# Layer-norm statistics behind a mixture in three parts, and POOL's share of the last norm in pieces of 256 columns

## The chip, the cores and the metric

The kernel runs on one core of a Trainium2 chip. The metric is the device time of one execution in microseconds (us). The engines are TensorE (PE, its weight loads are PEld), VectorE (DVE), ScalarE (ACT), GpSimd (POOL) and SyncE (SP), which here only issues DMA transfers.

## What is computed

Two decoder layers over 256 tokens of width 1024, batch 1, in float32. Layer 0 mixes the tokens with a sparse attention, layer 1 with a latent attention; both add a cross-attention into 256 memory tokens. Each half layer ends in a post-norm with residual, and each layer has a mixture of 16 experts. In short:

```python
DEEPNORM_ALPHA = (2.0 * DEPTH) ** 0.25
def layer_norm(x, g, b):
    mu = jnp.mean(xf, -1, keepdims=True)
    var = jnp.mean(jnp.square(xf - mu), -1, keepdims=True)
    y = (xf - mu) * lax.rsqrt(var + LN_EPS) * g + b
for i in range(DEPTH):
    ...
    x = layer_norm(DEEPNORM_ALPHA * x + y, ln_g[i, 0], ln_b[i, 0])
    f = hier_moe(x, moe_w_grp[i], moe_b_grp[i], moe_w_exp[i], moe_b_exp[i], moe_w_gate[i], moe_w_up[i], moe_w_down[i])
    x = layer_norm(DEEPNORM_ALPHA * x + f, ln_g[i, 1], ln_b[i, 1])
```

The change concerns the last line: the norm behind a mixture, once between the layers and once at the end of the kernel.

## The kernel before

**Tiles.** The 256 tokens are two tiles (t = 0, 1) of 128 partitions; the 1024 columns are two halves (h = 0, 1) of 512. `x_tm[:, t, h*512:...]` in SBUF holds the residual stream. The order of the instructions on each engine is the order in which the program writes them.

**The mixture** (`moe`) goes over eight pairs of experts (k = 0 to 7). For each pair PE multiplies by the gate and up matrices (`up`, L1606), then by the down matrix (L1780, for the last pair L1801). The outcome `yb` is split into a rounded part (ACT, L1807) and the rest (DVE, L1810), and `combine` (L1612, matmuls at L1615) adds both parts into `acc[t][hf]`, one PSUM bank of 512 columns for each tile and half. `acc[t][1]` already holds the residual of half 1, put in by PE (`add_x`), so half 1 is finished by matmuls alone; half 0 is added to `x_tm` by DVE (`resid`, L868), which also takes its statistics (`half_stats`, L875).

**The end of a mixture.** For the last pair, half 1 of the down product is done in two column blocks of 256, each with a PSUM bank of its own. Then DVE takes the statistics of half 0 of tile 1 (L1811), and PE issues `combine(7, 1, ...)` for columns 0 to 255 and 256 to 511: eight matmuls of 256 columns, in each block the rounded part for tiles 0 and 1, then the rest for tiles 0 and 1. `overflow` (L1625) follows: it loads a flag, and a block of code (L1637) runs only when an expert has too many tokens; every engine that has work in it passes the branch. From then on `z_(t, 1)` reads half 1 from `acc[t][1]`.

**The norm behind it.** `half_stats` writes six numbers per half into `lnst[t]`; `ln_stats` combines them (DVE, L908), adds epsilon (DVE, L909), and POOL raises the variance to the power -1/2 (L910) and makes the bias (L911). `norm` is two DVE instructions per half tile (L916, which needs the mean, and L917, which needs POOL's power). `norm_slow` does one half tile with ACT (L931) and two POOL instructions (L932 multiplies by the gain, L934 adds the bias).

**Between the layers** (`mla`, L1893 on): statistics of half 1 of tile 0, its norm, twelve warming matmuls on PE (`warm(12)`, L487), PE's transposes of that half tile (`xT`, L942), four more warming matmuls, then the same for tile 1, with the projection of layer 1 (L1888) behind the transposes.

**At the end** (`finish`, L2055): statistics of both tiles, `norm` of half 0 of tile 0, `norm_slow` of half 1 of tile 0, `norm` of half 0 and half 1 of tile 1. Each quarter of the output goes out by one DMA on SP's queue, in the order (0,0), (1,0), (0,1), (1,1), written as (tile, half); (0,1) is POOL's quarter.

Of the kernel before, what the change touches and what calls it, by code (L numbers as in the profile page):

```python
# [10 lines left out]
F32 = mybir.dt.float32  # L11
# [4 lines left out]
OP = mybir.AluOpType  # L16
# [3 lines left out]
P = 128  # L20
S = 256
D = 1024
NT = S // P
# [9 lines left out]
ALPHA = 4.0 ** 0.25  # L33
LN_EPS = 1e-5
# [74 lines left out]
def trunk(ctx: ExitStack, tc: tile.TileContext, A, out, dbg=None, layers=2, kb=ARENA_KB):  # L109
    nc = tc.nc  # L110
    PE, V, SC, G = nc.tensor, nc.vector, nc.scalar, nc.gpsimd
# [5 lines left out]
    work = ctx.enter_context(tc.tile_pool(name="work", bufs=2))  # L117
# [98 lines left out]
    def bank(name="pt"):  # L216
        return ps.tile([P, 512], F32, tag="ps", name=name)
# [420 lines left out]
    class Step:  # L638
# [46 lines left out]
        def norm(self, i):  # L685
            n0, sm = self.n0, self.sm[i]
            for t in range(NT):
                a, n = (0, n0) if t == 0 else (n0, S)
                v = self.p[i][:, a:a + n]
                if self.act:  # L690
                    SC.activation(v, v, AF.Copy, scale=sm[:, t:t + 1])
                else:
                    V.tensor_scalar(v, v, sm[:, t:t + 1], None, op0=OP.mult)
# [169 lines left out]
    lnst = {}  # L863

    def resid(t, h, yb, stats=True, f=ALPHA):

        z = x_tm[:, t, h * 512:(h + 1) * 512]
        V.scalar_tensor_tensor(z, z, f, yb, op0=OP.mult, op1=OP.add)  # L868
        if h == 0:
            lnst[t] = work.tile([P, 2, 6], F32, tag="lnst", name="lnst")  # L870
        if stats:
            half_stats(t, h)

    def half_stats(t, h):
        V.bn_stats(lnst[t][:, h, :], z_(t, h))  # L875

    def router_prep(l):

# [23 lines left out]
    def z_(t, h):  # L902
        return zps[t] if h and t in zps else x_tm[:, t, h * 512:(h + 1) * 512]

    def ln_stats(t, eps=LN_EPS):

        mv = lnmv[t] = work.tile([P, 5], F32, tag="lnmv", name="lnmv")
        V.bn_aggr(mv[:, 0:2], lnst[t])  # L908
        V.tensor_scalar(mv[:, 2:3], mv[:, 1:2], eps, None, op0=OP.add)  # L909
        G.tensor_tensor(mv[:, 3:4], mv[:, 2:3], mhalf, op=OP.pow)  # L910
        G.tensor_scalar(mv[:, 4:5], mv[:, 0:1], mv[:, 3:4], -1.0, op0=OP.mult, op1=OP.mult)  # L911
# [16 lines left out]
    def norm_slow(t, h, gb):  # L928

        z, mv = x_tm[:, t, h * 512:(h + 1) * 512], lnmv[t]  # L930
        SC.activation(z, z_(t, h), AF.Identity, bias=mv[:, 4:5], scale=mv[:, 3:4])  # L931
        G.tensor_tensor(z, z, gb[h][:, 0, :], op=OP.mult)  # L932
        yield
        G.tensor_tensor(z, z, gb[h][:, 1, :], op=OP.add)  # L934
        yield

    def xT(t, put, halves=(0, 1)):

# [420 lines left out]
    def out_tail(l):  # L1359
# [32 lines left out]
        for t in range(NT):  # L1392
            g_piece(l, 1, "b", 0, t)
            resid(t, 0, y[t, 0])
        for t in range(NT):
            xT(t, put, (0,))
            g_piece(l, 1, "b", 1, t)
        open_spare()
        resid(0, 1, y[0, 1])
        router(0, 0)  # L1400
        xT(0, put, (1,))
        resid(1, 1, y[1, 1], False)
        ln_stats(0)
        half_stats(1, 1)
        ln_stats(1)
        router(1, 0)
        xT(1, put, (1,))
# [99 lines left out]
    def moe(l, lg, lb, nxt):  # L1507
# [30 lines left out]
        def by4(v):  # L1538
            return v.rearrange("p (q c) -> p c q", c=4)
# [72 lines left out]
        def combine(k, hf, a=0, b=512):  # L1612
            for n in range(2):
                for t in range(NT):
                    PE.matmul(acc[t][hf][:, a:b], SkT[k % 2][:, t * P:(t + 1) * P], yhl[hf][n][:, a:b],  # L1615
                              start=(k == 0 and n == 0), stop=(k == 7 and n == 1 and b == 512), skip_group_check=True)
# [8 lines left out]
        def overflow():  # L1625


            go, gn = tmp("go", [P, NT, NE]), tmp("gn", [P, NT, NE - 1])
            xT = [tmp("oxT%d" % t, [P, KC, P]) for t in range(NT)]
            wt = [tmp("owt%d" % i, [P, 4, P]) for i in range(2)]  # L1630
            ho = tmp("ho", [P, S])
            wd = tmp("owd", [P, D])
            xs = tmp("oxs", [P, 512])
            zs = [tmp("ozs%d" % t, [P, 512]) for t in range(NT)]
            pg, yo = bank("pg"), bank("yo")
            flag = nc.values_load(over[0:1, 0:1], min_val=0, max_val=1)
            with tc.If(flag > 0):  # L1637
                V.scalar_tensor_tensor(go, rank, float(CAP), g16, op0=OP.is_gt, op1=OP.mult)
                for t in range(NT):
                    for c0 in range(0, KC, 4):  # L1640
                        xh, xl = [v[:, t, c0 * P:(c0 + 4) * P].bitcast(F32) for v in two[0]]
                        V.tensor_tensor(by4(xs), *[v.rearrange("p (c q) -> p c q", c=4) for v in (xh, xl)], op=OP.add)
                        for c in range(4):
                            PE.transpose(yo[:, c * P:(c + 1) * P], xs[:, c * P:(c + 1) * P], ident)
                        V.tensor_copy(xT[t][:, c0:c0 + 4, :], yo.rearrange("p (c t) -> p c t", c=4))
                    V.tensor_copy(zs[t], acc[t][1])
                with tc.For_i(0, NE, 1) as e:
                    with tc.For_i(0, FF // P, 1) as f:
                        for n, w in enumerate((A["moe_w_gate"], A["moe_w_up"])):
                            for hf in range(2):  # L1650
                                nc.sync.dma_start(wt[hf], w[l, bass.ds(e, 1), hf * 512:(hf + 1) * 512, bass.ds(f * P, P)]
                                                  .rearrange("o (c p) f -> p (o c) f", p=P))
                                for t in range(NT):
                                    for c in range(4):
                                        PE.matmul(pg[:, n * S + t * P:n * S + (t + 1) * P], wt[hf][:, c, :],
                                                  xT[t][:, 4 * hf + c, :], start=(n + hf + t + c == 0),
                                                  stop=(hf + c == 4), skip_group_check=True)
                        SC.activation(ho, pg[:, 0:S], AF.Silu)
                        V.tensor_tensor(ho, ho, pg[:, S:], op=OP.mult)
                        nc.sync.dma_start(wd, A["moe_w_down"][l, bass.ds(e, 1), bass.ds(f * P, P), :]  # L1660
                                          .rearrange("o p f -> p (o f)"))
                        for t in range(NT):
                            for hf in range(2):
                                z = zs[t] if hf else x_tm[:, t, 0:512]
                                PE.matmul(yo, ho[:, t * P:(t + 1) * P], wd[:, hf * 512:(hf + 1) * 512], start=True, stop=True)
                                V.scalar_tensor_tensor(z, yo, go[:, t, 0:1], z, op0=OP.mult, op1=OP.add)

                    V.tensor_copy(gn, go[:, :, 1:NE])
                    V.tensor_copy(go[:, :, 0:NE - 1], gn)
                for t in range(NT):  # L1670
                    V.tensor_copy(acc[t][1], zs[t])
                    half_stats(t, 0)
            ar.drop("go", "gn", "oxT0", "oxT1", "owt0", "owt1", "ho", "owd", "oxs", "ozs0", "ozs1")

        places(0)
# [17 lines left out]
        for k in range(8):  # L1693
# [52 lines left out]
            if k == first - 1:  # L1746
# [4 lines left out]
                for j in range(first, 8):  # L1751
                    i = j % 2
                    at[j] = (two[1][:, :, 2 * i:2 * i + 2, :],
                             lambda c, i=i: x2[c // 4][:, c % 4, i * P:(i + 1) * P])
# [55 lines left out]
                        V.tensor_tensor(yhl[hf][1][:, cs], yb[:, cs], yhl[hf][0][:, cs].bitcast(F32), op=OP.subtract)  # L1810
        half_stats(1, 0)  # L1811
        ar.drop("Sk", "Skg", "xg0", "h_sb")
        for a in (0, 256):
            combine(7, 1, a, a + 256)
        for t in range(NT):
            zps[t] = acc[t][1]

        overflow()
        ar.drop("rank", "g16")
# [34 lines left out]
    def mla(res):  # L1854
# [13 lines left out]
        gb = res["gb"]  # L1868
# [21 lines left out]


        SC.activation(kTb[0][:, 0, 0:1], mhalf, AF.Exp)
        half_stats(0, 1)  # L1893
        ln_stats(0, LN_EPS / ALPHA ** 2)
        norm(0, 0, gb)
        warm(12)
        xT(0, put, (0,))
        warm(4)
        split("mi1", hi=(SC, SC), lo=(None, None))
        half_stats(1, 1)  # L1900
        ln_stats(1, LN_EPS / ALPHA ** 2)
        split("mi1", hi=(None, None), lo=(G, G))
        norm(1, 0, gb)
        norm(0, 1, gb)
# [150 lines left out]
    def finish(res):  # L2055

        ov = out[0].rearrange("(t p) d -> p t d", p=P)
        gb = res["gb"]

        def put(t, h, z):  # L2060
            nc.sync.dma_start(ov[:, t, h * 512:(h + 1) * 512], z)

        for t in range(NT):
            half_stats(t, 1)
            ln_stats(t, LN_EPS / ALPHA ** 2)
        put(0, 0, norm(0, 0, gb))
        slow = norm_slow(0, 1, gb)
        next(slow)
        put(1, 0, norm(1, 0, gb))
        next(slow)  # L2070
        put(0, 1, x_tm[:, 0, 512:])
        put(1, 1, norm(1, 1, gb))
# [37 lines left out]
```

## Time and profile before

| | us |
|---|---|
| runs | 723.64, 723.23, 722.20 (median 723.23) |
| the profiled execution's own time | 723.13 |
| its span | 721.3 |
| PE busy | 695.8 (96%) |
| DVE, ACT, POOL busy | 278.8, 218.1, 157.7 |
| bytes moved by DMA | 235.58 MB, mean 327 GB/s |

The span runs from the first to the last record of the profile; the execution's own time lies 1.8 us above it. Busy time is the sum of an engine's instructions. Matmuls are pipelined, so a busy PE is not PE at its peak.

### The profile page before, as it was taken

To read this page: it belongs to the slowest core of one execution; us is meant where nothing else is said; L and a number is where in the kernel's file an instruction comes from. 1 tells how busy PE (TensorE), PEld (TensorE's weight loads), DVE (VectorE), ACT (ScalarE), POOL (GpSimd) and SP (SyncE) were. 2 spreads that over 40 slices of the span, in tenths; PEclk is the share of its full clock that TensorE was granted. 3 is DMA by queue.
4 is the path that set the end of the run, shared out by engine and by line. 5 is a ranking of instruction groups with operands and counts; after the bars stand their busy time and mean duration, and the time that the engine had idled before them with its cause. 6 is when DMAs were issued, how large, how long until landed. Compare 5 with 4: busy or idle time off the path is not lost. (4 is left out here: it accounts for less than half of the span.)

```text
span 721.3 us, 10956 instructions
## 1 busy us (share of the span) xinstructions
PE 695.8 (96%) x4122; PEld 414.5 (57%) x4122; DVE 278.8 (39%) x730; ACT 218.1 (30%) x528; POOL 157.7 (22%) x249
## 2 busy tenths in 40 slices
PE   7999999899999999999999999999999999999993
PEld 7999998777543435335344677776435334353342
DVE  4255587857621221021112776646403111211206
ACT  3365457673412101010121754443203011111011
POOL 5998645031301300000000640032103000000003
PEclk9999999999999999999999999999999999999997
DMA  9895875537879999999999994567899999999971
GB/s 298 255 277 167 277 296 165 216 146 276 310 274 420 387 383 417 419 421 420 419 419 369 389 408 164 205 237 266 342 364 420 418 419 420 422 418 418 420 245 60
DMA packets 66728, 235.58 MB, mean 327 GB/s; under 512 B 10923, under 2 KB 30446, under 8 KB 47214
## 3 DMA queue, kind: packets, MB, share of 16 engines
q1 hardware_dynamic: 66670, 234.82, 84.4%
q8 instruction: 34, 0.56, 0.3%
q14 instruction: 24, 0.20, 0.1%
HBM read 233.76 MB, written 1.05 MB: 326 GB/s over the span
## 5 line engine op out<-in xcount | busy, mean ns | idle before, releaser
L384 POOL TENSOR_TENSOR wl<-arena,wh 128x256 fp32r<-128x256 f32 (+4 forms) x108 | 91.2, 882 | 23.7 <-ACT wh L374 6.7
L1780 PE MATMUL yb<-arena 128*64 128x512 f32 x328 | 88.7, 595 | 0.0
L910 POOL TENSOR_TENSOR lnmv<-lnmv,mhalf 128x1 f32<-128x1 f32 x8 | 6.4, 805 | 359.6 <-DVE lnmv L909 359.3
L1730 DVE SCALAR_TENSOR_TENSOR arena<-arena,csb,u 128x512 f32<-128x512 f32 x16 | 12.0, 748 | 187.8 <-PE u L1606 106.7
L1606 PE MATMUL g<-arena 128*64 128x512 f32 x196 | 53.8, 593 | 0.0
L1785 DVE TENSOR_TENSOR y<-yb,y 128x512 fp32r<-128x512 f32 x28 | 19.4, 692 | 85.4 <-ACT y L1784 85.4
L1780 PEld LDWEIGHTS yb<-arena 128*64 128x64 f32 x328 | 27.3, 137 | 42.1 <-issue 40.9
L1606 PE MATMUL u<-arena 128*64 128x512 f32 x180 | 48.8, 593 | 0.0
L675 ACT ACTIVATE arena<-s,mx 128x128 f32<-128x128 f32 (+1 forms) x88 | 36.9, 430 | 35.2 <-DVE mx L669 35.2
L1784 ACT CAST y<-yb 128x512 fp32r<-128x512 f32 x28 | 16.4, 585 | 89.7 <-PE yb L1780 89.7
L1742 ACT COPY arena<-hT 128x256 f32<-128x256 f32 x16 | 6.0, 372 | 117.2 <-DVE arena L1742 117.2
L1606 PE MATMUL g<-arena,xg 128*64 128x512 f32 x144 | 39.7, 592 | 0.0
L1606 PE MATMUL u<-arena,xg 128*64 128x512 f32 x168 | 39.6, 592 | 0.0
L1780 PE MATMUL yb<-split,arena 128*64 128x512 f32 x112 | 39.4, 596 | 0.0
L1615 PE MATMUL acc<-y,SkT 128*128 128x512 f32 (+1 forms) x136 | 38.6, 406 | 0.0
L1720 ACT ACTIVATE arena<-g 128x512 f32<-128x512 f32 x16 | 9.6, 597 | 92.1 <-PE g L1606 92.0
L1615 PEld LDWEIGHTS acc<-y,SkT 128*128 128x128 f32 x136 | 22.6, 189 | 15.9 <-issue 12.9
L669 DVE TENSOR_REDUCE mx<-s 128x1 f32<-128x128 f32 (+1 forms) x88 | 27.2, 363 | 9.8 <-PE s L653 4.9
L1606 PEld LDWEIGHTS g<-arena 128*64 128x64 f32 x196 | 16.8, 137 | 23.3 <-issue 22.4
L1606 PEld LDWEIGHTS u<-arena 128*64 128x64 f32 x180 | 15.1, 137 | 23.6 <-issue 23.6
L1551 POOL TENSOR_TENSOR xl<-x_tm,xh 128x512 fp32r<-128x512 f32 x8 | 12.0, 1549 | 68.9 <-ACT xh L1550 68.9
L374 ACT CAST wh<-arena 128x1024 fp32r<-128x1024 f32 (+3 forms) x26 | 25.1, 999 | 3.8 <-DMA arena<-in_mem_w_kv_dram 2.8
(417 smaller groups left out, 1367.9 us busy)
## 6 DMA issues: line engine op xcount, KB each, us to landing
arena<-in_moe_w_down_dram SPq DMA_DIRECT2D x41, 1024.0 KB, 11.5
arena<-in_moe_w_up_dram SPq DMA_DIRECT2D x41, 1024.0 KB, 15.7
arena<-in_moe_w_gate_dram SPq DMA_DIRECT2D x35, 1024.0 KB, 15.6
arena<-in_moe_w_gate_dram SPq DMA_DIRECT2D x31, 512.0 KB, 7.8
split<-in_moe_w_down_dram SPq DMA_DIRECT2D x14, 1024.0 KB, 17.3
split<-in_moe_w_gate_dram SPq DMA_DIRECT2D x13, 1024.0 KB, 14.6
arena<-in_nsa_w_in_dram SPq DMA_DIRECT2D x7, 1024.0 KB, 8.0
arena<-in_moe_w_up_dram SPq DMA_DIRECT2D x14, 512.0 KB, 5.3
```

The costliest lines, as they stand in the source:

```text
L374: SC.copy(wh[:, c, :], t[:, c, :])
L384: lo[j].tensor_tensor(wl[:, d, :], t[:, d, :], wh[:, d, :].bitcast(F32), op=OP.subtract)
L669: V.tensor_reduce(self.mx[i][:, t:t + 1], v, axis=AX.X, op=OP.max, negate=True)
L675: SC.activation(self.p[i][:, a:a + n], self.sb[i][:, a:a + n], AF.Exp, bias=self.mx[i][:, t:t + 1], scale=1.0, accum_out=self.sm[i][:, t:t ...
L1551: G.tensor_tensor(zl, z, zh.bitcast(F32), op=OP.subtract)
L1606: PE.matmul(b_[e * 64:(e + 1) * 64, :], at[k][1](i * n + c)[:, e * 64:(e + 1) * 64], w_[e][:, c, :], start=(i + c == 0), stop=(i * n + c = ...
L1615: PE.matmul(acc[t][hf][:, a:b], SkT[k % 2][:, t * P:(t + 1) * P], yhl[hf][n][:, a:b], start=(k == 0 and n == 0), stop=(k == 7 and n == 1 a ...
L1720: SC.activation(h_sb, gp, AF.Silu)
L1730: V.scalar_tensor_tensor(h_sb, h_sb, gs[:, k % 2:k % 2 + 1], up_, op0=OP.mult, op1=OP.mult)
L1780: PE.matmul(yb[hf][e * 64:(e + 1) * 64, :], hT[:, 2 * q + c, e * 64:(e + 1) * 64], w_[e][:, c, hf * 512:(hf + 1) * 512], start=(q + c == 0 ...
L1784: SC.copy(yhl[hf][0], yb[hf])
L1785: V.tensor_tensor(yhl[hf][1], yb[hf], yhl[hf][0].bitcast(F32), op=OP.subtract)
```

## The change

Statistics of half 1 behind a mixture are taken in two instructions of 256 columns instead of one of 512, so `lnst[t]` has three groups of six numbers. Those of columns 0 to 255 stand directly behind the closing matmuls of these columns, in front of the matmuls of columns 256 to 511 and in front of the branch; those of columns 256 to 511 stay where the statistics of 512 were. In `norm_slow` POOL's multiplication and addition are each written as two instructions of 256 columns. Both layers have the first edit, the last norm alone the second.

```diff
-            lnst[t] = work.tile([P, 2, 6], F32, tag="lnst", name="lnst")
+            lnst[t] = work.tile([P, 3, 6], F32, tag="lnst", name="lnst")
...
-    def half_stats(t, h):
-        V.bn_stats(lnst[t][:, h, :], z_(t, h))
+    def half_stats(t, h, part=None):
+
+        i, z = (h, z_(t, h)) if part is None else (1 + part, z_(t, h)[:, part * 256:part * 256 + 256])
+        V.bn_stats(lnst[t][:, i, :], z)
...
-    def ln_stats(t, eps=LN_EPS):
+    def ln_stats(t, eps=LN_EPS, n=2):
...
-        V.bn_aggr(mv[:, 0:2], lnst[t])
+        V.bn_aggr(mv[:, 0:2], lnst[t][:, 0:n])
...
         SC.activation(z, z_(t, h), AF.Identity, bias=mv[:, 4:5], scale=mv[:, 3:4])
-        G.tensor_tensor(z, z, gb[h][:, 0, :], op=OP.mult)
-        yield
-        G.tensor_tensor(z, z, gb[h][:, 1, :], op=OP.add)
-        yield
+        for k, op in enumerate((OP.mult, OP.add)):
+            for c in (slice(0, 256), slice(256, 512)):
+                G.tensor_tensor(z[:, c], z[:, c], gb[h][:, k, c], op=op)
+            yield
...
                     V.tensor_copy(acc[t][1], zs[t])
                     half_stats(t, 0)
+                    half_stats(t, 1, 0)
...
         half_stats(1, 0)
         ar.drop("Sk", "Skg", "xg0", "h_sb")
-        for a in (0, 256):
-            combine(7, 1, a, a + 256)
         for t in range(NT):
             zps[t] = acc[t][1]
+        combine(7, 1, 0, 256)
+        for t in range(NT):
+            half_stats(t, 1, 0)
+        combine(7, 1, 256, 512)
...
-        half_stats(0, 1)
-        ln_stats(0, LN_EPS / ALPHA ** 2)
+        half_stats(0, 1, 1)
+        ln_stats(0, LN_EPS / ALPHA ** 2, 3)
         norm(0, 0, gb)
         warm(12)
...
-        half_stats(1, 1)
-        ln_stats(1, LN_EPS / ALPHA ** 2)
+        half_stats(1, 1, 1)
+        ln_stats(1, LN_EPS / ALPHA ** 2, 3)
...
         for t in range(NT):
-            half_stats(t, 1)
-            ln_stats(t, LN_EPS / ALPHA ** 2)
+            half_stats(t, 1, 1)
+            ln_stats(t, LN_EPS / ALPHA ** 2, 3)
```

## Rows read from the trace of the kernel before

**Rows 1.** Busy time by stretch: PE, PEld, DVE, ACT, POOL, PE clock, DMA share, GB/s.

```profile
610.00:630.00 20.00, 20.00 (x96) 7.77 (x94) 2.87 (x6) 1.92 (x4) 0.00 (x0) 1.00 1.01 421
```

**Rows 2.** Waits of PEld, 404 to 710 us: total us, times, longest.

```profile
PEld yb L1780 <- DMA arena<-in_moe_w_up_dram: 0.3, 1, 0.3
```

**Rows 3.** Timeline of DVE at the end: start us, us, line, operation, out<-in, [idle before <-releaser].

```profile
708.73 0.42 DVE L1810 TENSOR_TENSOR y<-yb,y 128x256 fp32r<-128x256 f32 x1
709.07 0.68 DVE L875 BATCH_NORM_STATS2 lnst<-x_tm 128x6 f32<-128x512 f32 x1
709.97 0.70 DVE L875 BATCH_NORM_STATS2 lnst<-acc 128x6 f32<-128x512 f32 x1 [0.21 <-DVEq L1637]
...
711.02 0.69 DVE L875 BATCH_NORM_STATS2 lnst<-acc 128x6 f32<-128x512 f32 x1
...
712.10 0.75 DVE L916 SCALAR_TENSOR_TENSOR x_tm<-x_tm,lnmv,arena 128x512 f32<-128x512 f32 x1
712.97 0.75 DVE L917 SCALAR_TENSOR_TENSOR x_tm<-x_tm,lnmv,arena 128x512 f32<-128x512 f32 x1
713.64 0.75 DVE L916 SCALAR_TENSOR_TENSOR x_tm<-x_tm,lnmv,arena 128x512 f32<-128x512 f32 x1
714.50 1.56 DVE L917 SCALAR_TENSOR_TENSOR x_tm<-x_tm,lnmv,arena 128x512 f32<-128x512 f32 x1
715.98 0.74 DVE L916 SCALAR_TENSOR_TENSOR x_tm<-acc,lnmv,arena 128x512 f32<-128x512 f32 x1
716.76 0.97 DVE L917 SCALAR_TENSOR_TENSOR x_tm<-x_tm,lnmv,arena 128x512 f32<-128x512 f32 x1
```

**Rows 4.** Timeline of POOL at the end.

```profile
711.18 0.55 POOL L910 TENSOR_TENSOR lnmv<-lnmv,mhalf 128x1 f32<-128x1 f32 x1 [160.64 <-DVE lnmv L909]
711.83 0.27 POOL L911 TENSOR_SCALAR lnmv<-lnmv 128x1 f32<-128x1 f32 x1
712.23 1.04 POOL L910 TENSOR_TENSOR lnmv<-lnmv,mhalf 128x1 f32<-128x1 f32 x1
713.36 0.49 POOL L911 TENSOR_SCALAR lnmv<-lnmv 128x1 f32<-128x1 f32 x1
713.82 1.70 POOL L932 TENSOR_TENSOR x_tm<-x_tm,arena 128x512 f32<-128x512 f32 x1
715.59 1.59 POOL L934 TENSOR_TENSOR x_tm<-x_tm,arena 128x512 f32<-128x512 f32 x1
```

**Rows 5.** GB/s of the DMA from 716 us to the end, in 40 equal slices.

```profile
GB/s 0 0 0 0 0 0 287 382 341 396 314 28 0 109 410 369 355 396 396 382 369 382 314 14 0 0 0 0 0 0 0 0 0 0 0 0 0 0 0 0
```

**Rows 6.** DVE by line and shape: count, busy us, mean ns, idle before.

```profile
L1810 DVE TENSOR_TENSOR y<-yb,y 128x256 fp32r<-128x256 f32 x4 | 1.7, 416 | 0.2
L1810 DVE TENSOR_TENSOR y<-yb,y 128x512 fp32r<-128x512 f32 x2 | 1.4, 692 | 10.0 <-ACT y L1807 10.0
```

**Rows 7.** Timeline of PE and PEld at the end: the closing matmuls of the mixture.

```profile
708.21 1.50 PE L1615 MATMUL acc<-y,SkT 128*128 128x256 f32 x8
...
709.21 0.30 PEld L1615 LDWEIGHTS acc<-y,SkT 128*128 128x128 f32 x2 [0.16 <-DVE y L1810]
```

**Rows 8.** Costliest groups, ACT's half of a copy out of one bank.

```profile
L1742 ACT COPY arena<-hT 128x256 f32<-128x256 f32 x16 | 6.0, 372 | 117.2 <-DVE arena L1742 117.2
```

**Rows 9.** Timeline at the boundary between the layers.

```profile
396.30 1.50 PE L1615 MATMUL acc<-y,SkT 128*128 128x256 f32 x8
...
398.48 2.75 PE L487 MATMUL warm<-onesb 128*128 128x512 bf16 x12 [0.68 <-PEq L1637]
...
400.34 0.75 DVE L917 SCALAR_TENSOR_TENSOR x_tm<-x_tm,lnmv,arena 128x512 f32<-128x512 f32 x1 [0.46 <-POOL lnmv L910]
...
401.21 0.42 PEld L942 LDWEIGHTS pt<-ident,x_tm 128*128 128x128 f32 x4 [0.47 <-issue]
```

**Rows 10.** POOL's split instructions at L384: ns min/median/max, first and last start, shapes.

```profile
L384 POOL TENSOR_TENSOR wl<-arena,wh x108: 717/746/1731, 10.0 to 423.4; 128x256 fp32r<-128x256 f32 x80, 128x420 fp32r<-128x420 f32 x8, 128x384 fp32r<-128x384 f32 x8, 128x512 fp32r<-128x512 f32 x8
```

## The prediction, made before the changed kernel was run

> **What bounds the kernel now.** I read the stretches first. In the second mixture TensorE (PE) is busy for 20.00 of 20 us while the weight DMA runs at full share [rows 1]; both look full, so the waits of PE's weight loads decide: from 404 to 710 us the only wait for a DMA is 0.3 us [rows 2]. PE's own work sets the pace there, and whatever delays PE in front of the second layer is paid in full. The change touches two places: the end of the kernel and the boundary between the layers, where the same instructions stand at another time.
>
> At the end the reader is to see in the DVE's timeline that DVE hardly rests: statistics of tile 1's first half at 709.07 to 709.75, the first statistics behind the mixture at 709.97, then everything back to back to 717.73, with one instruction (714.50) that takes 1.56 us and one (716.76) that takes 0.97 where their like take 0.75 [rows 3]. POOL's timeline says why [rows 4]. Its power of tile 1 starts at 712.23 and takes 1.04 us, against 0.55 for tile 0: it ends 0.42 us after DVE's instruction of 712.10 ends (712.85). Its bias of 713.36 ends 0.13 after DVE's of 712.97 ends (713.72). The multiplication of 713.82 ends 1.13 us after DVE's of 713.64 ends (714.39); the DVE instruction of 714.50, which waited meanwhile, ends 0.54 us after that multiplication. So a DVE instruction with two operands in SBUF and a POOL instruction exclude each other for their whole length, and POOL asks 0.13 us after its recorded start (0.55 less 0.42). DVE's 715.98, which reads the PSUM bank, takes its usual 0.74 beside POOL. Last, the two closing output transfers move 512 KB in ten slices of 0.13 us, 717.7 to 719.0 [rows 5]: the first begins 0.5 us behind POOL's end at 717.18, and they end 1.3 us behind DVE's end at 717.73. SP issues them in program order, POOL's quarter first.
>
> **The change, part by part.**
>
> *Price of a 256-column statistics instruction.* None is in the trace. With 512 columns it takes 0.68 to 0.70 us [rows 3]; the DVE subtraction takes 692 ns at 512 and 416 at 256 [rows 6], 0.28 less. I take 0.42. The ends are 0.35 (half) and 0.69 (no cheaper). Four of them replace two of 0.69: 0.30 us more DVE work.
>
> *The two early ones.* They stand behind DVE's 709.07 and in front of the branch. DVE has no idle time there: its gap is 709.75 to 709.97, 0.22 us, put down to the queue's branch. An independent instruction starts 0.08 us before the one in front ends (713.64 against 713.72 [rows 3]), so the early ones run 709.67 to 710.09 and 710.01 to 710.43. The columns they read are ready: four of the eight closing mixture matmuls need them, all eight are issued from 708.21, and the last two start at 709.21, released by DVE's subtraction [rows 7].
>
> *A new wait on PE.* The other four matmuls write the other half of the same accumulator banks, and now stand behind DVE's reads in the program. Does PE wait? Rows show how this program treats two engines on halves of one bank: DVE copies the left half of hT and ACT the right half, neither needs the other, yet what ends the idle time in front of ACT's 16 copies (117.2 us) is DVE's copy, not the transposes that fill the bank [rows 8]. I take it that banks are ordered whole, so PE waits. The second of the four (tile 1) cannot start before 710.43, plus 0.06 from DVE to PE (709.15 to 709.21 [rows 3, 7]): 710.49. From there two matmuls take 0.50 and each more 0.15 (two loads in 0.30) [rows 7]: PE ends at 710.49 + 0.65 = 711.14 instead of 709.71, 1.43 later; tile 0's part ends at 710.99. Bounds: no wait at all, 0; by the price of the statistics (0.35 and 0.69), 1.29 and 1.97.
>
> The Trainium skill has a rule against this change, on the page "PSUM — Partial Sum Buffer", section "PSUM bank collisions raise a hardware error": two engines in one bank and quadrant at once raise an error even at different columns and nothing arbitrates, so software must guard the whole bank. By it the wait has to be there, and the time is the 726.8 below; without it, 725.3. No row here shows matmuls against reads; the copies show two readers.
>
> *The boundary.* The same four matmuls ended there at 397.80, PE's twelve warming matmuls began 0.68 later, at 398.48, and the transposes of the normalized tile at 401.21, 2.73 behind that [rows 9]. Shifted by 1.43: 397.80 to 399.23, 399.91, 402.64. DVE's side is hidden under it: its last operation for these transposes ended at 401.09, and moves by 1.13 (start of the first remaining statistics, next paragraph) less 0.27, to 401.95. **Boundary: +1.43**, and by rows 1 and 2 it stays to the end. Cover gone (no warming matmuls in the way), it would be 0.86.
>
> *The end: statistics.* The first remaining statistics start with PE's 710.99 and a hand-over of 0.06 to 0.2, say 711.10, against 709.97. The third group adds six numbers to the combining instruction: nothing, against its neighbours. From there DVE's first normalization came 2.13 later (712.10); two shorter records take off 0.54, so it starts at 712.69. Call that moment A: 712.10 before, +0.59.
>
> *The end: POOL in pieces.* POOL's power for tile 0 came 1.21 behind the first statistics, now 0.94: 712.04 to 712.59, its bias 0.10 later at 712.69 and asking at 712.82. DVE takes the port at A = 712.69; before, the bias was done when A came. So POOL is put behind one more DVE instruction. With before's distances on DVE and 0.42 or 0.13 us behind DVE's ends for POOL's small ones: bias ends A+0.88; power of tile 1, blocked by DVE's second instruction (A+0.87 to A+1.62), ends A+2.04; its bias, blocked by the third, ends A+2.42. DVE's fourth starts at A+2.40 and no longer waits: it ends A+3.15, saving 0.81. A POOL piece of 256 columns takes 0.72 alone [rows 10], 0.59 behind a release: the first ends A+3.74. The second starts 0.07 later, as between POOL's two now (715.52 to 715.59), and would ask at A+3.94, but DVE's last has the port from A+3.85 to A+4.60 (0.78 behind the start of the one that reads PSUM, A+3.07). The pieces then end at A+5.19, A+5.98 and A+6.77, 719.46. Before, POOL ended at 717.18 = A+5.08 and DVE at A+5.63. DVE now ends 1.03 us sooner in its own count, POOL 1.69 later, and POOL is what the output waits for. Both closing transfers now queue behind it: 719.46 + 0.5 + 1.3 = 721.26, against 719.03. **End: +2.2**, of which 0.59 is the later A. Two of these orders hang on 0.13 and 0.09 us; the other way they give back 0.5 and 0.35.
>
> *Nothing:* two more semaphore pairs on POOL and two more instructions in the untaken branch have no row that ends a wait.
>
> **Sum.** 1.43 + 2.2 = 3.6 us on the profiled run's own 723.13 (its span is 721.3): 726.8. The median of the three runs, 723.23, is 0.1 above it. With the statistics at 0.35 the sum is 3.2, at 0.69 5.3.
>
> **Rivals.**
> 1. *PE does not wait.* For: no row has matmuls against a reader. Against: rows 8. Then the remaining statistics start 0.22 behind 710.43, at 710.65; the boundary costs 0.68 less 0.27 = 0.41 and A moves by 0.14: the end costs 1.75. 725.3.
> 2. *The weight stream paces the second mixture*, and the boundary's 1.43 vanishes. For: DMA share 1.01 at 421 GB/s [rows 1]. Against: rows 2. 723.13 + 2.2 = 725.4.
> 3. *POOL's pieces slip between DVE's* (the other side). Place: the last norm; it decides whether POOL's fourth piece ends before DVE's last instruction. If POOL is not locked out, it starts at A+1.72 as before (713.82) and needs four times 0.72 and three gaps of 0.07: A+4.81, beside DVE at some A+4.85; the transfers then end at A+4.81 + 1.8 = A+6.6 against A+6.9: 0.3 gained. For: DVE's waits of 0.81 and 0.22 are there to be had. Against: POOL was locked out in rows 4 each time. With PE's wait, 1.43 + 0.59 - 0.3 = 1.7: 724.8. Without, 0.41 + 0.14 - 0.3 = 0.25: 723.4, not slower; if the early statistics also cost half, 0.35, a little under the time before.
>
> **How the numbers follow.** A measurement of this kernel tells about 0.2% from no change, 1.4 us: 721.8 and 724.7 bound "same". Forecast 0.48 (own range 726.0 to 728.2, from the orders that give back and the dearer statistics); rival 1 0.15; rival 2 0.08; rival 3 with the wait 0.10, half of it beyond 724.7; rival 3 without 0.19, of which 0.07 under 721.8 for gains that I don't see. Slower 0.48 + 0.15 + 0.08 + 0.05 = 0.76, same 0.05 + 0.12 = 0.17, faster 0.07. The range leaves out rival 3 without the wait: 723.8 to 728.2.
>
> **What would show it.** In the changed profile: 256-column statistics near 0.42 us; the last mixture matmuls of both layers starting behind DVE's second early statistics, some 1.4 us later against the subtraction in front; the boundary's transposes 1.4 later against it too; at the end DVE's last instruction done about 2 us before POOL's fourth piece, and both closing transfers behind POOL. It is wrong if PE's last four matmuls run beside DVE's early statistics, if POOL's pieces end before DVE, or if the shift at the boundary is gone by the last mixture.

## The result, and the profile after

The changed kernel takes 728.02 us (median of 6 runs, 725.63 to 728.43) against 723.15 before (6 runs, 722.20 to 723.64): ratio 1.0060, 95% interval 1.0048 to 1.0072. It is slower, by more than the 726.8 forecast and inside the range. Four of its runs lie at 727.93 to 728.43 with a mean granted clock of 0.988 to 0.990, two at 725.63 and 726.15 with 0.993. Two executions of the kernel before in later rounds, of 741.11 and 2484.46 us, count as slow and are left out of every ratio and range below. The profiled run takes 728.37 us with a span of 726.5, which is 5.2 over before's 721.3.

To see where, I count each profile from two marks: DVE's statistics of tile 1's first half at the boundary (b0) and at the last mixture (b1). No instruction that the change adds lies in front of b0. T is the first transpose of the normalized tile on PE, "warm" what the twelve warming matmuls in front of it take.

```
                   b0      b0 to T  warm   T to b1  b1 to span's end  span
before             397.16  4.08     2.75   307.83   12.23             721.3
after              398.32  6.79     4.44   307.91   13.48             726.5
difference         +1.16   +2.71    +1.69  +0.08    +1.25             +5.2
```

The rows of b0 and T, before and then after (T of the changed kernel stands in the next rows):

```profile
397.16 0.68 DVE L875 BATCH_NORM_STATS2 lnst<-x_tm 128x6 f32<-128x512 f32 x1
401.24 0.63 PE L942 MATMUL pt<-ident,x_tm 128*128 128x128 f32 x4
```

```profile
398.32 0.68 DVE L877 BATCH_NORM_STATS2 lnst<-x_tm 128x6 f32<-128x512 f32 x1
```

So 1.16 us came ahead of the change, 2.71 at the boundary (1.43 forecast), nothing in the second mixture, 1.25 at the end (2.2 forecast).

PE's timeline of the changed kernel, at the boundary and at the end (start us, us, line, operation, [idle before <-releaser]):

```profile
399.48 0.87 PE L1617 MATMUL acc<-y,SkT 128*128 128x256 f32 x4 [1.28 <-DVE lnst L877]
400.84 4.44 PE L487 MATMUL warm<-onesb 128*128 128x512 bf16 x12 [0.49 <-PEq L1639]
405.11 0.60 PE L944 MATMUL pt<-ident,x_tm 128*128 128x128 f32 x4
...
714.18 0.86 PE L1617 MATMUL acc<-y,SkT 128*128 128x256 f32 x4 [1.29 <-DVE lnst L877]
```

The forecast wait is there in both layers: PE's last four mixture matmuls, which were part of one unbroken group of eight [rows 7, 9], now stand 1.28 and 1.29 us behind DVE's early statistics. What was not forecast is the next line: the twelve warming matmuls take 4.44 us, not 2.75 [rows 9]. The windows view (PE, PEld, DVE, ACT, POOL busy, PE clock, DMA share, GB/s) says why; after first, then before:

```profile
130.00:135.00 5.00, 3.81 (x22) 2.75 (x22) 3.20 (x12) 3.63 (x13) 0.00 (x0) 0.66 0.72 297
401.00:405.10 4.10, 4.10 (x12) 1.55 (x11) 3.12 (x8) 0.28 (x2) 2.89 (x4) 0.59 1.03 404
```

```profile
130.00:135.00 5.00, 4.58 (x41) 3.86 (x42) 3.61 (x14) 3.65 (x14) 0.00 (x0) 1.00 0.82 300
...
398.48:401.20 2.72, 2.72 (x12) 1.08 (x12) 2.19 (x6) 0.98 (x2) 1.82 (x2) 1.00 1.05 411
```

PE is busy all through the warming matmuls in both kernels, but the granted clock is 0.59 after and 1.00 before: behind its standstill PE ran most of them at 1.2 GHz in place of 2.4. The first rows show the same in the first layer, where the program did not change: 0.66 against 1.00. That fall is only a part of the 1.16, as the same matmuls around it show, before and then after:

```profile
127.23 1.08 PE L1198 MATMUL ob<-arena 90*64 90x256 f32 x8
130.41 1.91 PE L720 MATMUL ob<-arena 128*64 128x256 f32 x16 [2.10 <-DVE arena L712]
```

```profile
128.03 1.08 PE L1200 MATMUL ob<-arena 90*64 90x256 f32 x8
131.19 2.73 PE L720 MATMUL ob<-arena 128*64 128x256 f32 x16 [2.08 <-DVE arena L712]
```

The changed kernel is 0.80 us late already ahead of the standstill, where the clock is full in both; behind the fall it is 1.75 late (at the statistics of the first layer's first norm, 174.57 against 172.82), and by b0 it has won back 0.59 of that. What makes the first 0.80 is not known.

DVE's and POOL's timelines of the changed kernel at the end:

```profile
713.02 0.69 DVE L877 BATCH_NORM_STATS2 lnst<-x_tm 128x6 f32<-128x512 f32 x1
713.62 0.75 DVE L877 BATCH_NORM_STATS2 lnst<-acc 128x6 f32<-128x256 f32 x2
714.97 0.43 DVE L877 BATCH_NORM_STATS2 lnst<-acc 128x6 f32<-128x256 f32 x1 [0.60 <-PE acc L1617]
...
716.62 0.77 DVE L918 SCALAR_TENSOR_TENSOR x_tm<-x_tm,lnmv,arena 128x512 f32<-128x512 f32 x1
...
719.03 1.03 DVE L919 SCALAR_TENSOR_TENSOR x_tm<-x_tm,lnmv,arena 128x512 f32<-128x512 f32 x1
719.98 0.74 DVE L918 SCALAR_TENSOR_TENSOR x_tm<-acc,lnmv,arena 128x512 f32<-128x512 f32 x1
720.75 1.12 DVE L919 SCALAR_TENSOR_TENSOR x_tm<-x_tm,lnmv,arena 128x512 f32<-128x512 f32 x1
```

```profile
716.58 0.27 POOL L913 TENSOR_SCALAR lnmv<-lnmv 128x1 f32<-128x1 f32 x1
716.81 0.99 POOL L912 TENSOR_TENSOR lnmv<-lnmv,mhalf 128x1 f32<-128x1 f32 x1
...
718.35 4.10 POOL L936 TENSOR_TENSOR x_tm<-x_tm,arena 128x256 f32<-128x256 f32 x4
```

POOL's third and fourth piece in rows of narrower windows:

```profile
720.60 1.85 POOL L936 TENSOR_TENSOR x_tm<-x_tm,arena 128x256 f32<-128x256 f32 x2
...
721.28 1.17 POOL L936 TENSOR_TENSOR x_tm<-x_tm,arena 128x256 f32<-128x256 f32 x1
```

A 256-column statistics instruction takes 0.43 us. DVE's first normalization is 3.60 behind b1, against 3.03 in rows 3. POOL's four pieces end at 722.45, 0.58 behind DVE's last (721.87); before, POOL ended 0.55 ahead of DVE [rows 3, 4]. The output transfers wait for that, in the GB/s line of 716 to 727 us (slices of 0.275 us):

```profile
GB/s 0 0 0 0 0 0 0 0 0 0 0 194 387 358 15 0 0 37 357 387 172 0 0 0 0 0 156 365 387 387 395 216 0 0 0 0 0 0 0 0
```

The last burst, both closing quarters in one, begins 0.5 us behind POOL's end.

### The profile page after: what moved, and what is told of

Read it like the earlier page. It is cut to its first block, busy times and chain, and to the rows that moved or that the text cites. A ratio compares the mean times of both kernels' runs of the same rounds, so it can differ in the third digit from the quotient of the medians.

```text
span 726.5 us, 10964 instructions
## 1 busy us (share of the span) xinstructions
PE 698.5 (96%) x4122; PEld 415.0 (57%) x4122; DVE 279.5 (38%) x734; ACT 218.4 (30%) x528; POOL 157.2 (22%) x251
## 3 DMA queue, kind: packets, MB, share of 16 engines
HBM read 233.76 MB, written 1.05 MB: 323 GB/s over the span
## 5 line engine op out<-in xcount | busy, mean ns | idle before, releaser
L384 POOL TENSOR_TENSOR wl<-arena,wh 128x256 fp32r<-128x256 f32 (+4 forms) x108 | 89.8, 869 | 27.7 <-ACT wh L374 9.6
```

The lines of the kernel that those rows point to most:

```text
L384: lo[j].tensor_tensor(wl[:, d, :], t[:, d, :], wh[:, d, :].bitcast(F32), op=OP.subtract)
```

## The experiments

Each went in rounds beside the kernel before, on the same chip; ratios are to that, and are not exactly the quotients of the medians. The kernel before had a median of 724.88 us in the rounds of experiments 1 to 4, 723.56 in those of 5 to 8 and 723.24 in those of 9 to 12, so the times of different groups are not to be set against each other.

**1. POOL's pieces alone**, in the kernel before.

```diff
-        G.tensor_tensor(z, z, gb[h][:, 0, :], op=OP.mult)
-        yield
-        G.tensor_tensor(z, z, gb[h][:, 1, :], op=OP.add)
-        yield
+        for k, op in enumerate((OP.mult, OP.add)):
+            for c in (slice(0, 256), slice(256, 512)):
+                G.tensor_tensor(z[:, c], z[:, c], gb[h][:, k, c], op=op)
+            yield
```

> Statistics as before, POOL's two instructions of the last norm in four pieces of 256 columns. My theory (POOL and DVE exclude each other for a whole instruction, the one that starts first goes first): nothing changes up to the last mixture, DVE's two long waits at the end (0.81 and 0.22 us) become some 0.3 each, POOL's last piece ends about 5.8 us behind DVE's first normalization (5.08 before, DVE 5.63), so that both closing transfers wait for POOL: the end is 0.6 to 0.9 us later than before, 723.8 to 724.1. Rival (the pieces slip between DVE's instructions and help): POOL ends before DVE and the end is 0.3 to 0.8 us earlier, 722.4 to 722.9.

725.44 us, ratio 1.0003 (0.9988 to 1.0017). In its profile the boundary is before's (4.08, warm 2.75) and the end takes 12.95, 0.72 more than before. So the pieces cost 0.72, too little for the ratio to show. b0 lies at 400.74, 3.6 later than before, with the same program in front of it: spans cannot be compared, stages can.

**2. The statistics alone**: the changed kernel with the diff of experiment 1 undone, so with POOL's instructions whole.

> Statistics in three parts as in the changed kernel, POOL's two instructions whole as before. My theory: both layers keep PE's wait of 1.3 us behind DVE's early statistics; at the boundary it costs 1.2 us directly and 1.5 more in runs in which the clock falls to half in the warming matmuls (their twelve take 4.4 instead of 2.75 us); at the end DVE's first normalization is 0.6 later and the rest is as before. 726.3 with the fallen clock, 724.8 without it; 0.7 us under the changed kernel. Rival (the pieces are what costs): within 0.5 us of before, 723.7.

728.29 us, 1.0043 (1.0029 to 1.0058). Boundary 6.79, end 12.79 (+0.56).

```profile
401.14 0.87 PE L1617 MATMUL acc<-y,SkT 128*128 128x256 f32 x4 [1.28 <-DVE lnst L877]
402.50 4.44 PE L487 MATMUL warm<-onesb 128*128 128x512 bf16 x12 [0.49 <-PEq L1639]
```

The statistics alone make the kernel slower, with the same standstill and the same slow matmuls. 0.56 and 0.72 add up to 1.28, the end's 1.25.

**3. No wait on PE.**

```diff
         combine(7, 1, 0, 256)
+        combine(7, 1, 256, 512)
         for t in range(NT):
             half_stats(t, 1, 0)
-        combine(7, 1, 256, 512)
```

> As the changed kernel, but the two early statistics stand behind both blocks of closing matmuls, so that PE has nothing to wait for; DVE does the same work in the same order. My theory (PE's wait and the clock are the cost, DVE's extra work is small): PE's last four matmuls run as before, the warming matmuls take 2.75 us at full clock, the boundary is 0.2 to 0.5 us later than before, the end 0.6 to 0.9: 724.0 to 724.5, in every run. Rival (DVE's work, two more instructions in front of the branch, is the cost): within 0.5 us of the changed kernel, 727.5 to 728.5.

727.56 us, 1.0030 (1.0016 to 1.0044). Boundary 4.95, 0.87 over before, end 13.28 (+1.05), both more than expected. DVE's timeline, then PE's:

```profile
401.56 0.43 DVE L877 BATCH_NORM_STATS2 lnst<-acc 128x6 f32<-128x256 f32 x1 [0.66 <-DVEq L1639]
```

```profile
400.81 2.75 PE L487 MATMUL warm<-onesb 128*128 128x512 bf16 x12 [0.61 <-PEq L1639]
404.50 0.63 PE L944 MATMUL pt<-ident,x_tm 128*128 128x128 f32 x4 [0.94 <-DVE x_tm L919]
```

No standstill, full clock, and yet 0.87: the transposes now wait for DVE. Its work in front of them grew by 0.42, as both tiles' early statistics lie there (the prediction's 0.30 was for all four), and its gap at the branch by 0.45, from 0.21 at the same place before to 0.66. DVE was hardly hidden under the warming matmuls before: its operation ended at 401.09, 0.12 ahead of the weight loads of the transposes [rows 9], the same distance as here.

**4. The wait stays, PE doesn't stand still** (the changed kernel, at the boundary only).

```diff
             half_stats(t, 1, 0)
+        if nxt:
+            warm(7)
         combine(7, 1, 256, 512)
```

> As the changed kernel, with seven warming matmuls more between the two blocks of closing matmuls of the first layer, so that PE works while it would wait. My theory (the clock falls because PE stands still for 1.3 us and again for 0.5): the clock stays up, the twelve warming matmuls take 2.75 us in every run, PE's last four matmuls start no later than in the changed kernel, and the time is 1.5 us under the changed kernel's longer runs: 726 to 726.7, with a spread under 1 us. Rival (the clock falls for another reason, or the longer time is not the clock's): as the changed kernel, 728, with two groups of runs.

727.75 us, 1.0036 (1.0023 to 1.0049); the spread of the runs, 726.23 to 728.75, is larger than expected. Boundary 5.10, warm 2.75, end 13.48.

```profile
399.75 1.68 PE L487 MATMUL warm<-onesb 128*128 128x512 bf16 x7
401.19 0.86 PE L1617 MATMUL acc<-y,SkT 128*128 128x256 f32 x4
402.54 2.75 PE L487 MATMUL warm<-onesb 128*128 128x512 bf16 x12 [0.49 <-PEq L1639]
```

The four matmuls still start 0.56 us behind the start of the early statistics, at 401.19, as in the changed kernel, but the clock doesn't fall, and the boundary is 1.69 shorter than after: 4.44 less 2.75. The wait at full clock costs 1.02.

**5. The order of the two closing transfers.**

```diff
-        put(0, 1, x_tm[:, 0, 512:])
         put(1, 1, norm(1, 1, gb))
+        put(0, 1, x_tm[:, 0, 512:])
```

> The changed kernel with one pair of lines exchanged: the transfer of DVE's last quarter (tile 1, second half) is issued on SP ahead of that of POOL's quarter (tile 0, second half). Counted from DVE's statistics of tile 1's first half to the end, where the changed kernel has 13.48 us. Theory (both closing transfers stand behind POOL's last piece because SP issues in program order, and each alone takes about half of the 1.3 us): DVE's quarter leaves at its end, 0.58 us before POOL's, and the stage falls by about 0.5, to 12.9 to 13.0. Rival (the closing transfers are bounded by something else, a fixed time behind POOL's end): 13.4 to 13.5. In the time of the whole kernel this is under 0.1%, so the stage decides.

727.57 us, 1.0046 (1.0030 to 1.0061), which can't show half a microsecond. The end takes 12.90 against 13.48, as the theory had it: DVE's quarter no longer waits in SP's queue behind POOL's. The profile shows a second thing, at the boundary, where the program is the changed kernel's:

```profile
401.34 0.85 PE L1617 MATMUL acc<-y,SkT 128*128 128x256 f32 x4 [1.28 <-DVE lnst L877]
402.69 2.75 PE L487 MATMUL warm<-onesb 128*128 128x512 bf16 x12 [0.50 <-PEq L1639]
405.28 0.60 PE L944 MATMUL pt<-ident,x_tm 128*128 128x128 f32 x4
```

The same standstill, and this time no fall: 5.10. The fall behind it is a matter of the run.

**6. Five warming matmuls for twelve**, at the boundary of the changed kernel.

```diff
-        warm(12)
+        warm(5)
```

> The changed kernel with five warming matmuls in place of twelve at the boundary, a stage that takes 6.79 us there from DVE's statistics to PE's transposes of the normalized tile (4.08 before the change). Theory (the twelve at half clock, 4.44 us, are what the transposes wait for, and DVE is ready at about 5.0): five at half clock take 1.9, and the transposes begin at 5.0 to 5.2, released by DVE. If the granted clock is still at its lower level then, the transposes and the projection behind them give some of the 1.7 back, which shows as a longer way from the transposes to the last mixture than 307.9. Rival (the boundary is bound by DVE or the queue's branch at 6.8, and the slow matmuls only fill that time): 6.7 to 6.8, with the transposes released by DVE.

728.08 us, 1.0049 (1.0030 to 1.0068): nothing gained. In the profile the clock didn't fall either (five took 1.24 us), so it doesn't test the slow ones; the transposes begin 4.87 behind b0, less than the 5.0 to 5.2 expected:

```profile
404.88 0.63 PE L944 MATMUL pt<-ident,x_tm 128*128 128x128 f32 x4 [1.13 <-DVE x_tm L919]
```

That is the limit of DVE's side, which holds 0.60 us of DVE's own waiting for PE's four matmuls; seven more warming matmuls at full clock add some 0.2 to it (5.10 in experiments 4 and 5).

**7. Gains and biases in PSUM** (the kernel before; three more banks written by PE in the last norm).

```diff
+        pb = []
+        for h in range(2):
+            for k in range(h, 2):
+                pt = bank()
+                for c in range(4):
+                    j = k * 32 + 24 + h * 4 + c
+                    PE.transpose(pt[:, c * P:(c + 1) * P], vcol[:, j:j + 1].to_broadcast([P, P]), ident)
+                pb.append(pt)
...
+            V.scalar_tensor_tensor(z, z_(t, h), mv[:, 0:1], gb[1][:, 0, :] if h else pb[0], op0=OP.subtract, op1=OP.mult)
+            V.scalar_tensor_tensor(z, z, mv[:, 3:4], pb[h + 1], op0=OP.mult, op1=OP.add)
```

> The kernel before the change, with one thing different in the last norm: PE, which has nothing to do there, spreads the gain of the first half and the biases of both halves into three PSUM banks, and DVE's normalizations read these, so that each has one operand in SBUF and not two. From DVE's statistics of tile 1's first half to the end, where the kernel before has 12.23 us and the changed one 13.48. Theory (what POOL and DVE lose there is the exclusion of each other's SBUF operands, 0.81 and 0.22 us on DVE and 0.5 on POOL's power): DVE runs beside POOL, POOL's power of tile 1 takes 0.55 again, and the stage takes 10.9 to 11.5; the kernel is then 0.7 to 1.3 us faster than before, 0.998 to 0.999 of it. Rival (PSUM operands are as dear, or the spreading by PE comes late): 12.0 to 12.4, no difference.

724.06 us, 0.9991 (0.9975 to 1.0007): the kernel's time alone doesn't show a gain. The end takes 11.06, 1.17 less than before. DVE, then POOL:

```profile
714.90 0.75 DVE L2071 SCALAR_TENSOR_TENSOR x_tm<-x_tm,lnmv,pt 128x512 f32<-128x512 f32 x1
...
716.41 0.75 DVE L2071 SCALAR_TENSOR_TENSOR x_tm<-x_tm,lnmv,pt 128x512 f32<-128x512 f32 x1
```

```profile
712.68 0.55 POOL L910 TENSOR_TENSOR lnmv<-lnmv,mhalf 128x1 f32<-128x1 f32 x1
...
713.55 1.27 POOL L932 TENSOR_TENSOR x_tm<-x_tm,arena 128x512 f32<-128x512 f32 x1
```

These took 1.56, 0.97, 1.04 and 1.70 before [rows 3, 4]. With one SBUF operand each on DVE, nobody waits: the exclusion was the end's cost. The Trainium skill ("SBUF — State Buffer", section "Who interferes with whom") says that a DVE instruction with two SBUF inputs contends with a GpSimd instruction that reads SBUF. The trace agrees: 1.56 us with two, 0.75 with one.

**8. One early statistic in place of two**, in the kernel of experiment 2: tile 0's alone, and ahead of the statistics of tile 1's first half. Stages count from it.

```diff
-        half_stats(1, 0)
...
         combine(7, 1, 0, 256)
-        for t in range(NT):
-            half_stats(t, 1, 0)
+        half_stats(0, 1, 0)
         combine(7, 1, 256, 512)
+        half_stats(1, 0)
...
-        half_stats(1, 1, 1)
-        ln_stats(1, LN_EPS / ALPHA ** 2, 3)
+        half_stats(1, 1)
+        ln_stats(1, LN_EPS / ALPHA ** 2)
```

> The changed kernel with POOL's instructions whole, and only tile 0 with statistics ahead of the branch: DVE takes the early 256 columns of tile 0 before the statistics of tile 1's first half, so that PE's last four mixture matmuls stand behind one early instruction, not two, and tile 1 takes its second half whole behind the mixture. Counted from the first of these DVE instructions. Theory (PE's standstill of 1.29 us is what lowers the granted clock): PE stands still for 0.3 to 0.6 us, the clock stays at its upper level, the twelve warming matmuls take 2.75 us and not 4.44, and the boundary costs 0.2 to 0.9 us over before's 4.08, not 2.71; the end costs 0.1 to 0.6. In all 0.3 to 1.5 us over before, 1.0005 to 1.002. Rival (the clock falls for another reason, such as the reads of DVE themselves): 4.4 us for the twelve, 1.003 to 1.005 in all.

724.95 us, 1.0022 (1.0005 to 1.0040). Boundary 4.29 (+0.21) and end 12.31 (+0.08), at and just under the low edge of what was expected; PE stood still for 0.69 us, a little more than expected. The ratio is higher than these 0.3 us, and b0 lay at 400.4.

```profile
400.95 0.71 PE L1617 MATMUL acc<-y,SkT 128*128 128x256 f32 x4 [0.69 <-DVE lnst L877]
402.08 2.75 PE L487 MATMUL warm<-onesb 128*128 128x512 bf16 x12 [0.42 <-PEq L1639]
```

**9 to 12. The first layer's standstill filled.** All ten kernels so far, before and after among them, let PE stand still for 2.1 us near 130 us. Behind it the clock was full in the profile of before and fell in the nine others so far, and b0 came up to 3.6 us later. Not all of that is the clock: ahead of the standstill these nine were already 0.1 to 2.5 us late (127.3 to 129.8 against 127.23). Eight warming matmuls there take the fall out of the comparison:

```diff
             pull(fills[j])
+            if j in idle:
+                warm(8)
             st.oget(st)
...
-        attention(steps, FILLS, extra, 3.0, lambda: first_pieces(0), (12,))
+        attention(steps, FILLS, extra, 3.0, lambda: first_pieces(0), (12,), (7,))
```

9, the kernel before with it:

> The kernel before, with eight warming matmuls put on PE into a standstill of 2.1 us that lies in the first layer (128.3 to 130.4 us of the span, PE waiting for DVE's copy of the transposed probabilities), far from the change and the same in both kernels. Behind it the granted clock is at its upper level in the profile of before and falls for 2 to 7 us in every other profile taken so far, so that the stages behind it start up to 3.5 us later. Theory (the standstill lets the clock fall in most runs): with the filler no fall is seen at 130 to 140 us, DVE's statistics at the boundary start at 396.8 to 397.4, and the times gather near the lowest of the kernel before: ratio 0.997 to 0.9995. Rival (the clock falls there for a reason that a filler doesn't touch, or the filler delays the matmuls behind it): the shifts stay and the ratio is 0.9995 to 1.002.

722.71 us (722.27 to 723.48), 0.9992 (0.9980 to 1.0004).

```profile
129.11 1.90 PE L487 MATMUL warm<-onesb 128*128 128x512 bf16 x8
131.28 1.91 PE L720 MATMUL ob<-arena 128*64 128x256 f32 x16 [0.27 <-DVE arena L712]
```

```profile
130.00:135.00 5.00, 4.73 (x38) 3.26 (x37) 3.60 (x14) 3.63 (x13) 0.00 (x0) 1.00 0.84 320
135.00:140.00 5.00, 5.00 (x39) 4.60 (x37) 3.54 (x14) 3.97 (x15) 0.00 (x0) 1.00 0.50 200
```

The clock stays up in this profile and in the three that follow, and the twelve runs lie within 1.2 us, where the 33 of before beside them spread over 5 (722.01 to 727.24, 14 of them above 723.48). In experiment 12, with the same filler, the twelve spread over 2.7. The ratio's interval still touches 1, and b0 still varies between these four profiles, from 396.91 to 397.77 (396.8 to 397.4 expected), though no clock falls ahead of it.

10, the changed kernel with it:

> The changed kernel with the same filler in the first layer, so that its distance to the kernel before with the filler is the change alone. Theory: where the clock stays up at the boundary, 1.02 us there and 1.25 at the end, 2.3 in all, 1.003 of the kernel before with the filler; where it falls behind PE's standstill of 1.29 us, 1.7 more, 4.0, 1.0055. As the first six runs of the changed kernel lay 4.9 us over before, I expect the fall in half of the runs or more, and 1.004 to 1.0055. Rival (the clock at the boundary is a rare event, and the rest of the 4.9 us came from the first layer): 1.0028 to 1.0035, and the runs lie close together.

726.09 us, 1.0048 (1.0034 to 1.0061); b0 397.17, boundary 6.78, end 13.53. Seven runs lie at 725.74 to 726.20 with a mean clock of 0.992 to 0.994, five at 727.20 to 727.75 with 0.990. The profile is of the five, and has the 4.44:

```profile
398.33 0.86 PE L1619 MATMUL acc<-y,SkT 128*128 128x256 f32 x4 [1.28 <-DVE lnst L879]
399.68 4.44 PE L487 MATMUL warm<-onesb 128*128 128x512 bf16 x12 [0.50 <-PEq L1641]
```

11, both fillers:

> The changed kernel with both fillers: that of the first layer, and the seven warming matmuls between DVE's early statistics and PE's last four mixture matmuls, so that PE's new wait stays but PE doesn't stand still. Theory: no fall of the clock in either place, 5.1 us from DVE's statistics to the transposes at the boundary, 13.5 at the end, 2.3 us over the kernel before with the filler: 1.003 of it, and 1 to 2 us under the changed kernel with the first filler alone. Rival (the fall at the boundary costs nothing in most runs): the same time as the changed kernel with the first filler.

726.08 us, 1.0035 (1.0022 to 1.0049); boundary 5.16, warm 2.75, end 13.51. Eleven of the twelve runs lie at 725.53 to 726.48: the upper group is gone (the twelfth, 727.47, has a clock of 0.994). The five over the seven are 1.5 us (means 727.43 and 725.91), near the 1.69 of the boundary. The medians of 10 and 11 don't differ, so the 1 to 2 us expected between them are not there and the rival has the median right: five of 10's runs, fewer than half, have the lower clock, and between the means the second filler is worth 0.5 us.

12, the candidate (7 with the filler):

> The kernel before with the filler of the first layer and with the gains and biases of the last norm in PSUM, the candidate for the fastest. Theory: the end takes 11.06 us as it did without the filler (12.23 before), 1.2 us under the kernel before with the filler, and no fall of the clock in the first layer: 0.9955 to 0.998 of the kernel before, whose runs lie at 722.3 to 727. Rival (either gain is lost again, in another standstill): 0.998 to 1.000.

721.54 us (720.90 to 723.58), 0.9975 (0.9962 to 0.9989): faster than the kernel before and the changed one. Its end takes 11.09, 12.13 in 9; the median is 1.17 under that of 9, and ten of the twelve runs lie below the lowest of 9.

## Why the prediction was right, and where its terms were off

**The price of the statistics: right.** 0.42 forecast, 0.43 measured; the third group of six costs 0.03 in the combining instruction.

**The wait on PE: right, and it is one for the whole bank.** The four matmuls end 1.39 us later against b0 (from 0.64 behind it [rows 9] to 2.03), 1.43 forecast. This was reasoned from two readers of one bank [rows 8]; the 1.28 us that PE stands behind DVE's reads of the other half is the row for matmuls. The Trainium skill's rule ("PSUM — Partial Sum Buffer", section "PSUM bank collisions raise a hardware error") asks for that wait. The trace agrees that the program has it; no run here shows what would happen with both engines in one bank at once. Rival 1 falls.

**"Shifted by 1.43" at the boundary: the term that was mis-sized.** Measured 2.71, for two reasons of opposite sign. At full clock the wait costs 1.02 (experiments 4 and 5; 1.09 between 9 and 11): the hand-over to the warming matmuls shrank from 0.68 to 0.49, and the transposes came 2.59 behind these and not 2.76 (both on PE; the 2.73 of the prediction is their weight loads), since before, DVE's end held them (0.12 in front of their loads, as in experiment 3, where they wait for DVE). So DVE's side was not hidden before, as the prediction had it. And the step took the twelve warming matmuls as 2.75 us whatever went before them. Behind PE's new standstill the clock falls in some runs: in three of the five profiles that have it (after, 2, 10; not 5, 6), in none of the three where it is filled or removed (3, 4, 11), nor behind 0.69 us in 8. A fall adds 1.69. That the standstill is what does it rests on these few profiles and on the upper group of 10's runs, which is gone in 11. The Trainium skill ("TensorE: Matmul & The Clock Gate", section "What's actually happening") says that the slow clock is the default and activity releases it; the trace agrees as far as it goes: 2.75 and 4.44 us for the same twelve, and no fall where PE was kept busy.

**The shift stays to the end: right.** From T to b1 all profiles have 307.6 to 308.0 us. Rival 2 falls.

**The end, 2.2 forecast and 1.25 measured.** A came 0.57 later against b1 (0.59 forecast). The failed step is that POOL was said to "ask" 0.13 us behind its recorded start and DVE at its own. POOL's bias started at 716.58, DVE's instruction at 716.62, and the bias went first, taking 0.27. The third piece started at 720.60 and took its 0.72 alone; DVE's last, at 720.75, waited (1.12 against 0.75). The prediction had the missing number: DVE's 714.50 ended 0.54 behind POOL's end, where it takes 0.75 alone, so it too asks some 0.21 behind its recorded start, and those that waited here ended 0.55 behind a piece. Counted on both sides, the bias (716.71 against 716.83) and the third piece (720.73 against 720.96) go first, as they did; DVE's 716.62, behind a bias that ended at 716.85, then takes 0.77, as measured. Both orders that the prediction called close (0.13 and 0.09 us) went the other way, and the 0.5 and 0.35 us came back: POOL ended at A+5.83, not A+6.77, DVE at A+5.25, not A+4.60. That both transfers queue behind POOL held, which experiment 5 shows.

**Rival 3** (the pieces slip between DVE's) came half true: the first and the third piece went ahead of a DVE instruction, which waited (1.03 and 1.12 us), and POOL still ended last. Only the third took 0.72, the others 1.16 or 1.17.

**The sum** was 3.6, the medians differ by 4.87. The range, up to 728.2, held with 0.2 us to spare, and that is in part luck: the errors had opposite signs (+1.28 at the boundary, -0.95 at the end), and in the profiled run 1.16 of the 5.2 came ahead of the change.

**Open.** Between 9 and 11, where no clock falls, the stages give 1.09 at the boundary, 0.24 from T to b1 and 1.38 at the end, 2.7 in all; the medians differ by 3.4. I don't know where the other 0.7 us lie: of their runs, the profiled ones are the highest (723.48) and one of the lowest (725.64). Why a fall comes in one run and not in the next with the same standstill was not tried.

## What to carry to other kernels

A wait costs its length only while it lasts: ask also what PE does next, at which granted clock, and whether cheap matmuls can fill the standstill. Splitting an instruction to start it earlier cost time here in both places, since PE on the same bank and DVE beside POOL were put behind it: look who that is before you split. Where DVE and POOL exclude each other, moving one of DVE's operands to PSUM gained 1.17 us at the end, where smaller pieces on POOL lost 0.72.

## What was unexpected of the hardware

- The clock behind an equal standstill (1.28 us) fell in one run and held in the next, and so did the one behind 2.1 us in the first layer: 0.66, 0.77 or 1.00 at 130 to 135 us in after, experiment 1 and before. With that standstill filled, the spread of before's runs fell from 5 us to 1.2 (2.7 in experiment 12).
- DVE's gap at the same untaken branch was 0.21 us before and 0.66 in experiment 3 at the boundary.
- DVE and POOL hold each other off only from a moment behind their recorded starts (an estimated 0.21 and 0.13 us, worked out above): a POOL instruction that began 0.04 us ahead of DVE's took its usual 0.27, and DVE's took 0.77, 0.02 more than alone.
